# Full 128 rows in place of 64 in one score matmul of an attention stage, on one core

## The chip, the cores and the metric

The kernel runs on one core of a Trainium2 chip. The metric is the device time of one execution in microseconds (us). A core has a matrix engine (TensorE, PE in the rows; its weight loads are listed apart as PEld), VectorE (DVE), ScalarE (ACT) and GpSimd (POOL); DMA queues are issued by SyncE (SP) and others. TensorE's clock has two levels, 1.2 and 2.4 GHz; the rows give the granted clock as a share of 2.4 GHz.

## What is computed

The reference is a backbone of two layers over 512 latent tokens of width 2048, with 256 context tokens ahead of them. Layer 0 is an attention layer with two groups of heads, layer 1 a Fourier mixing layer. The part that matters here is the first group of layer 0, eight latent heads ("A"). Their queries and keys have a part of 128 without position (nope) and a part of 64 with rotary position (pe); the rotary key is shared by all heads:

```python
def mla_qk(q_nope, q_pe, k_nope, k_pe):
    b, l, h, _ = q_nope.shape
    q = jnp.concatenate([q_nope, q_pe], axis=-1)[:, :, :, None, :]
    k = jnp.concatenate([k_nope, jnp.broadcast_to(k_pe, (b, l, h, A_ROPE))], axis=-1)
    return q, k
...
        sc = jnp.einsum("bqgrd,bkgd->bgrqk", qi, k, preferred_element_type=jnp.float32) * scale
        p = jax.nn.softmax(sc, axis=-1).astype(v.dtype)
        return jnp.einsum("bgrqk,bkge->bqgre", p, v)
```

There are 512 queries (four blocks of 128) against 256 + 512 = 768 keys. The second group, eight heads with normed queries and two key heads ("B"), has no such split.

## The kernel before

All data is float32. To keep its precision, each operand of a matmul is split into a high half (rounded to the type that TensorE multiplies, fp32r) and a low half, the rest. A product is then three matmuls, high by high, high by low and low by high (mm3, lines 56 to 59); low by low is left out. A split is a cast on ScalarE and a subtraction on VectorE (lines 39 to 46). Every matmul is issued by line 54 behind a load of its weights, the stationary operand.

The stages in order are: norms and projections of the tokens, the attention of layer 0 (function attention, line 692), its output projection, and the Fourier layer. In the attention stage the order of TensorE's work is that of the code (pinned, line 900). A loop over 64 steps (line 912), one step for each head and block of 128 queries, does for step i: the projections that later heads need (fills: q_nope, k_nope, q_pe, v_a), the transposes of the softmax of step i (turn), the product with the values of step i - 2 (values), and the scores of step i + 2 (scores). Steps 0 to 31 are the A heads, 32 to 63 the B heads. From step 27 on the scores stand ahead of the transposes. The second half of k_nope stands in the late table (line 920): in an even step ahead of the value product, in an odd one behind it, so that the next head's scores follow at once. The opening (lines 908 and 909) has the same sequence: the second half of k_nope, then scores; with the three odd steps there are four such places.

One score block (function score, lines 844 to 849) makes a tile S of 128 queries by 768 keys, in two segments of 512 and 256 columns. For each segment there are five matmuls: two for the rotary part, three for the nope part. For the rotary part, the query tile st (stk in the rows; line 806) of a head has 128 rows: in one half of the rows the high half of the 64 rotary query values, in the other half the low half of the same values; for even heads the high half is in rows 0 to 63, for odd heads in rows 64 to 127. The rotary key is stored twice, in rows 0 to 63 and in rows 64 to 127, and split into self.kpe[0] (high, kpeh in the rows) and self.kpe[1] (low, kpel). The first matmul, over all 128 rows, gives (high + low) query by high key. The second takes only the 64 rows with the high query, r to r + 63, by the low key. The nope part is qh, ql by kh, kl.

Behind a score block come the maximum (VectorE), the exp (ScalarE), the reciprocal (VectorE), the scaling (GpSimd, tile pm) and, two steps later, six transposes (pt).

A product of a B head is the nope part alone, six matmuls per block with 128 rows.

Of the kernel before, what the change touches and what calls it, by code (L numbers as in the profile page):

```python
# [24 lines left out]
class Build:  # L25
# [666 lines left out]
    def attention(self, keep):  # L692
        nc, d = self.nc, self.d
        self.y_d = [self.dr.tile([128, 512], F32, name=f"y{h}") for h in range(16)]
        with ExitStack() as s:
# [25 lines left out]
            def weight(src, k, n):  # L721
                raw = rawp.tile([128, 1024], F32, name="raw")
                r = raw[:, :k * n]
                self.load(r.rearrange("p (k c) -> p k c", k=k), src)
                hi = pg.tile([128, 1024], F32R, name="pgh")
                lo = pg.tile([128, 1024], F32R, name="pgl")
                self.split(r, hi[:, :k * n], lo[:, :k * n])
                return [(hi[:, n * i:n * i + n], lo[:, n * i:n * i + n]) for i in range(k)]

            def gemm(ps, lhs, rhs):  # L730
                n = len(lhs)
                for i in range(n):
                    self.mm3(ps, lhs[i], rhs[i], i == 0, i == n - 1)
                return ps

            def cut(p, a, b):
                return p[0][:, a:b], p[1][:, a:b]

            def pair(shape, tag, bufs=2):
                return (ap.tile(shape, F32R, name=tag + "h", bufs=bufs), ap.tile(shape, F32R, name=tag + "l", bufs=bufs))  # L740
# [58 lines left out]
            parts = {}  # L799
# [31 lines left out]
            def k_nope(h, part):  # L831
                if part == 0:
                    parts["kw"] = weight(d["wkn"][h], 4, 128)
                    parts["k", h] = pair([128, 768], "k")
                w, kn = parts["kw"], parts["k", h]
                a, b = segs[part]
                ps = acc.tile([128, 512], F32, name="acc")[:, :b - a]
                gemm(ps, w, [cut(c, a, b) for c in self.ckv])
                self.split(ps, *cut(kn, a, b))
                if part == 0:  # L840
                    return
                qn, st, r, i = parts["q", h], parts["st", h // 2][h % 2], 64 * (h % 2), h % 2

                def score(ps, qt):
                    o = 128 * qt
                    for a, b in segs:
                        self.mm(ps[:, a:b], st[:, o:o + 128], self.kpe[0][:, a:b], True, False)
                        self.mm(ps[:, a:b], st[r:r + 64, o:o + 128], self.kpe[1][r:r + 64, a:b], False, False)
                        self.mm3(ps[:, a:b], cut(qn, o, o + 128), cut(kn, a, b), False, True)
                heads[h] = {"score": score, "col": 0, "v": lambda t: [v[:, t, 128 * i:128 * i + 128] for v in parts["v", h // 2]]}  # L850

# [30 lines left out]
            for hp in range(4):  # L882
                b, n = 8 * hp, hp + 1
                if hp:
                    fills[b + 1] = [(q_nope, 2 * hp + 1)]
                fills[b + 2] = [(k_nope, 2 * hp + 1, 0)]
                late[b + 2] = (k_nope, 2 * hp + 1, 1)
                if n < 4:
                    fills[b + 3] = [(q_pe, n)]
                    fills[b + 4] = [(q_nope, 2 * n)]  # L890
                    fills[b + 5] = [(k_nope, 2 * n, 0)]
                    late[b + 5] = (k_nope, 2 * n, 1)
                    for t in range(3):
                        fills[b + 6 + t] = [(v_a, n, t)]
# [807 lines left out]
```

## Time and profile before

| | us |
|---|---|
| median of three runs | 2356.12 (2350.45 to 2357.21) |
| the profiled execution | 2353.7 |
| its span, first to last instruction | 2351.9 |
| TensorE busy | 2173.0 (92%) |
| VectorE busy | 1887.2 (80%) |
| ScalarE busy | 948.2 (40%) |
| GpSimd busy | 428.3 (18%) |

In the profiled execution the first score matmul of an A head starts at 643.06 us and the last at 870.16; the B heads follow to 960. The rows further down are of four views: busy time of each engine in a stretch; instructions in order of time (start and duration); groups of instructions by operands, with their mean duration and the idle time of their engine just before them; and the page of the profile. In a name like `S<-kpel,stk 64*128 64x512` the output tile stands first, then the moving and the stationary operand, the rows by columns of the weights, and the rows by columns of the moving operand. A matmul's bar overlaps the next one's; how fast the engine goes is read from the starts.

### The profile page before, as it was taken

Reading aid. Unit: us, or ns where it says so; the run is one execution under the profiler, and the core shown is the slowest. Engines: PE = TensorE matmul, PEld = TensorE weight load, DVE = VectorE, ACT = ScalarE, POOL = GpSimd, SP = SyncE. Lnnn points to the kernel's source line nnn. Section 1 sums busy time; section 2 is a strip of 40 time slices with the busy share of each in tenths; the row PEclk is TensorE's granted clock in tenths of the full one; section 3 lists DMA queues with packets and bytes.
Section 4 is the critical chain, followed back from the end, with each engine's and each line's share of the span. In section 5 each row is a group of like instructions: output and inputs, shape, how many; then the busy total and the mean of one; then the engine's idle time right before and its main releaser. Section 6 shows DMA issues by size and latency. Waiting matters only on the chain. (4 is left out here: it accounts for less than half of the span.)

```text
span 2351.9 us, 39267 instructions
## 1 busy us (share of the span) xinstructions
PE 2173.0 (92%) x15708; PEld 1998.8 (85%) x15708; DVE 1887.2 (80%) x2603; ACT 948.2 (40%) x1321; POOL 428.3 (18%) x407
## 2 busy tenths in 40 slices
PE   5999989989899999999978898998999998998994
PEld 3779879889888889877758898998999998998994
DVE  5456799998755569677889998779998999879898
ACT  2222344433443457422464333445344435445331
POOL 1023413100111113100252222001221224002003
PEclk9999989999999999999999999999999999999997
DMA  8852344666511122588536675535555456536332
GB/s 339 311 192 100 126 164 159 202 219 203 203 42 57 59 75 71 181 294 281 184 116 224 247 276 186 174 132 187 179 174 174 164 173 214 185 127 247 130 135 116
DMA packets 128702, 412.63 MB, mean 175 GB/s; under 512 B 14852, under 2 KB 15492, under 8 KB 126728
## 3 DMA queue, kind: packets, MB, share of 16 engines
q1 hardware_dynamic: 113144, 359.04, 44.7%
q0 software_dynamic: 8320, 31.33, 3.7%
q10 hardware_dynamic: 7056, 19.76, 2.2%
q8 instruction: 123, 2.02, 0.3%
q14 instruction: 59, 0.48, 0.1%
HBM read 347.81 MB, written 62.26 MB: 174 GB/s over the span
## 5 line engine op out<-in xcount | busy, mean ns | idle before, releaser
L54 PE MATMUL r<-bth,wl 128*128 128x256 f32 x1848 | 524.3, 284 | 16.0 <-DVE wl L44 15.7
L54 PE MATMUL r<-bth,wh 128*128 128x256 f32 x1848 | 525.6, 284 | 0.0
L54 PE MATMUL r<-btl,wh 128*128 128x256 f32 x1848 | 524.3, 284 | 1.3 <-DVE btl L44 1.0
L41 ACT CAST wh<-wraw 128x1024 fp32r<-128x1024 f32 x262 | 274.7, 1050 | 395.8 <-PE r L54 284.5
L44 DVE TENSOR_TENSOR wl<-wraw,wh 128x1024 fp32r<-128x1024 f32 x262 | 336.7, 1289 | 52.5 <-ACT wh L41 52.3
L54 PEld LDWEIGHTS r<-bth,wl 128*128 128x128 f32 x1848 | 352.1, 191 | 18.5 <-DVE wl L44 18.5
L54 PEld LDWEIGHTS r<-btl,wh 128*128 128x128 f32 x1848 | 351.1, 190 | 2.1 <-DVE btl L44 1.2
L54 PEld LDWEIGHTS r<-bth,wh 128*128 128x128 f32 x1848 | 351.5, 190 | 0.5 <-issue 0.5
L41 ACT CAST wh<-ws 128x1024 fp32r<-128x1024 f32 x183 | 191.8, 1049 | 339.9 <-PE r L54 321.4
L44 DVE TENSOR_TENSOR wl<-ws,wh 128x1024 fp32r<-128x1024 f32 x183 | 229.6, 1255 | 12.2 <-ACT wh L41 10.0
L197 DVE SCALAR_TENSOR_TENSOR mac<-macraw,cs,mac 128x512 f32<-128x512 f32 x240 | 193.6, 807 | 12.4 <-DMA macraw<-in_ada 11.0
L54 PE MATMUL r<-hlh,wl 128*128 128x256 f32 (+1 forms) x480 | 148.4, 309 | 31.8 <-DVE wl L44 31.7
L54 PE MATMUL r<-hlh,wh 128*128 128x256 f32 (+1 forms) x480 | 147.2, 307 | 0.1
L54 PE MATMUL r<-hll,wh 128*128 128x256 f32 (+1 forms) x480 | 145.8, 304 | 0.0
L54 PE MATMUL r<-bah,wl 128*128 128x256 f32 x384 | 113.3, 295 | 25.3 <-DVE wl L44 25.3
L54 PEld LDWEIGHTS r<-hlh,wl 128*128 128x128 f32 x480 | 94.7, 197 | 38.6 <-DVE wl L44 35.7
L41 ACT CAST pgh<-raw 128x512 fp32r<-128x512 f32 (+2 forms) x104 | 65.9, 660 | 124.2 <-DMA raw<-in_wo 51.4
L54 PE MATMUL r<-bah,wh 128*128 128x256 f32 x384 | 112.0, 292 | 0.0
L54 PE MATMUL r<-bal,wh 128*128 128x256 f32 x384 | 111.9, 291 | 0.0
L54 PE MATMUL oacc<-pgl,yh 128*128 128x512 f32 x256 | 103.1, 403 | 8.8 <-DVE pgl L44 8.8
L54 PE MATMUL r<-bbh,wl 128*128 128x256 f32 x384 | 108.6, 283 | 2.7 <-DVE wl L44 2.7
L54 PE MATMUL r<-bcl,wh 128*128 128x256 f32 x384 | 108.6, 283 | 1.5 <-DVE bcl L44 0.9
(489 smaller groups left out, 5707.4 us busy)
## 6 DMA issues: line engine op xcount, KB each, us to landing
macraw<-in_ada SPq DMA_DIRECT2D x72, 512.0 KB, 6.3
wraw<-in_win SPq DMA_DIRECT2D x66, 512.0 KB, 7.2
raw<-in_adas SPq DMA_DIRECT2D x64, 512.0 KB, 5.6
wraw<-in_wg SPq DMA_DIRECT2D x64, 512.0 KB, 6.9
wraw<-in_wu SPq DMA_DIRECT2D x64, 512.0 KB, 4.3
wraw<-in_wo SPq DMA_DIRECT2D x64, 512.0 KB, 4.6
macraw<-in_ada SPq DMA_DIRECT2D x112, 256.0 KB, 3.9
raw<-in_wo SPq DMA_DIRECT2D x40, 512.0 KB, 4.9
```

The costliest lines, as they stand in the source:

```text
L41: ins = nc.scalar.copy(out=hi, in_=src)
L44: sub = (eng or nc.vector).tensor_sub(out=lo, in0=src, in1=hi.bitcast(F32))
L54: self.pin(self.nc.tensor.matmul(ps, lhsT=a, rhs=b, start=start, stop=stop))
L197: ins = nc.vector.scalar_tensor_tensor(out=acc, in0=raw[:, k, :], scalar=col, in1=acc, op0=ALU.mult, op1=ALU.add)
```

## The change

The second rotary matmul takes all 128 rows of st and of the low key in place of the 64 rows from r. It so adds the product of the low query half and the low key, which was left out before. The variable r goes. Nothing else is changed; the instructions of every engine stand in the same order as before.

```diff
-                qn, st, r, i = parts["q", h], parts["st", h // 2][h % 2], 64 * (h % 2), h % 2
+                qn, st, i = parts["q", h], parts["st", h // 2][h % 2], h % 2
...
                     for a, b in segs:
                         self.mm(ps[:, a:b], st[:, o:o + 128], self.kpe[0][:, a:b], True, False)
-                        self.mm(ps[:, a:b], st[r:r + 64, o:o + 128], self.kpe[1][r:r + 64, a:b], False, False)
+                        self.mm(ps[:, a:b], st[:, o:o + 128], self.kpe[1][:, a:b], False, False)
                         self.mm3(ps[:, a:b], cut(qn, o, o + 128), cut(kn, a, b), False, True)
```

## Rows read from the trace of the kernel before

**Rows 1.** The page: span of the profiled execution and its instructions.
```profile
span 2351.9 us, 39267 instructions
```

**Rows 2.** Busy time by stretch (start:end, length, engines, PEclk, DMA share, GB/s): A heads, B heads.
```profile
642.90:870.30 227.40, 227.40 (x1335) 185.88 (x1334) 127.55 (x248) 97.51 (x190) 35.60 (x40) 1.00 0.18 56
870.30:960.10 89.80, 89.80 (x681) 85.50 (x680) 79.53 (x186) 63.75 (x137) 33.23 (x40) 1.00 0.29 95
```

**Rows 3.** TensorE in order of time (start us, duration us), one score block of an A head.
```profile
705.65 0.39 PE L54 MATMUL S<-kpeh,stk 128*128 128x512 f32 x1
705.97 0.50 PE L54 MATMUL S<-kpel,stk 64*128 64x512 f32 x1
706.40 0.50 PE L54 MATMUL S<-kh,qh 128*128 128x512 f32 x1
706.74 0.40 PE L54 MATMUL S<-kl,qh 128*128 128x512 f32 x1
...
707.20 0.28 PE L54 MATMUL S<-kpeh,stk 128*128 128x256 f32 x1
707.41 0.38 PE L54 MATMUL S<-kpel,stk 64*128 64x256 f32 x1
707.72 0.39 PE L54 MATMUL S<-kh,qh 128*128 128x256 f32 x1
707.94 0.28 PE L54 MATMUL S<-kl,qh 128*128 128x256 f32 x1
...
708.19 0.28 PE L54 MATMUL acc<-pgh,ckv0h 128*128 128x256 f32 x1
```

**Rows 4.** TensorE in order of time, one score block of a B head.
```profile
872.24 0.40 PE L54 MATMUL S<-kl,qh 128*128 128x512 f32 x1
872.47 0.39 PE L54 MATMUL S<-kh,ql 128*128 128x512 f32 x1
872.70 0.28 PE L54 MATMUL S<-kh,qh 128*128 128x256 f32 x1
872.82 0.28 PE L54 MATMUL S<-kl,qh 128*128 128x256 f32 x1
...
873.06 0.82 PE L775 MATMUL pt<-ident,pm 128*128 128x128 f32 x6
```

**Rows 5.** Weight loads by operands, A heads (count, busy us, mean ns, idle before, releaser).
```profile
L54 PEld LDWEIGHTS S<-kl,qh 128*128 128x128 f32 x64 | 12.1, 189 | 0.0
...
L54 PEld LDWEIGHTS S<-kh,qh 128*128 128x128 f32 x64 | 11.9, 186 | 11.9 <-issue 7.5 <-ACT pgh L41 0.2
L54 PEld LDWEIGHTS S<-kpel,stk 64*128 64x128 f32 x64 | 11.7, 183 | 15.7 <-issue 15.7
```

**Rows 6.** TensorE in order of time, startup: narrow matmuls (psa), then full ones.
```profile
37.27 1.07 PE L301 MATMUL psa<-raw,cs 128*32 128x256 f32 x16
38.27 0.50 PE L54 MATMUL psl<-hlh,pgh 128*128 128x512 f32 x1
38.61 0.40 PE L54 MATMUL psl<-hll,pgh 128*128 128x512 f32 x1
38.85 0.40 PE L54 MATMUL psl<-hlh,pgl 128*128 128x512 f32 x1
```

**Rows 7.** All engines in order of time: a score directly behind k_nope's second half.
```profile
691.37 0.40 PE L54 MATMUL S<-kpeh,stk 128*128 128x512 f32 x1
691.49 0.83 ACT L41 CAST pgh<-raw 128x768 fp32r<-128x768 f32 x1 [1.75 <-issue]
...
693.23 0.42 DVE L44 TENSOR_TENSOR kl<-acc,kh 128x256 fp32r<-128x256 f32 x1
...
693.66 0.28 PE L54 MATMUL S<-kl,qh 128*128 128x256 f32 x1
```

**Rows 8.** All engines in order of time: a scaled softmax tile, and the transposes reading it.
```profile
863.68 0.91 POOL L761 TENSOR_SCALAR pm<-pm,rs 128x768 f32<-128x768 f32 x1 [9.34 <-DVE nb L754]
...
866.01 0.82 PE L775 MATMUL pt<-ident,pm 128*128 128x128 f32 x6
```

## The prediction

> **What bounds the kernel now.** I read the time before from the outside in. The span is 2351.9 us [rows 1]; the profiled execution took 2353.7 us with what lies around the span, and the median of the three runs shown is 2356.12, 2.4 us more. The change touches one instruction of the score product of the eight A heads, so the second view is the busy time in the stretch that holds these heads, from the first score matmul to the last, beside the stretch of the B heads behind it. In the A stretch TensorE is busy for all of the 227.40 us, VectorE for 127.55, ScalarE for 97.51, GpSimd for 35.60, the DMA share is 0.18, and the granted clock is 1.00, that is 2.4 GHz throughout [rows 2]. So nothing but TensorE sets the end of this stretch: what its instructions give up here moves everything behind it. The B stretch reads the same way (89.80 of 89.80 us), and there all score matmuls have 128 rows.
>
> But busy is not the same as fast: a matmul's bar includes its wait for the array. So the third view is the order in time, read by starts and not by bars. One query block of an A head is ten matmuls, five on 512 columns and five on 256. Their starts stand at 705.65, 705.97, 706.40 and 706.74, then at the start of the 256 part at 707.20, 707.41, 707.72, 707.94, and the next work starts at 708.19 [rows 3]. The steps are 0.32, 0.43, 0.34 and then 0.23 each in the first half; 0.21, 0.31, 0.22 and then 0.12 or 0.13 in the second. In a B head, where the form never changes, a step is 0.23 for 512 columns and 0.12 for 256 [rows 4]. The extra time thus stands around the 64-row matmul alone: before it, behind it, and once more behind the first full matmul that follows.
>
> The fourth view, weight loads grouped by operands, says how. The loads of the 64-row step (kpel,stk) take 183 ns each, hardly less than the 189 ns of a full one, and the load engine stood idle for 15.7 us before them, put down to "issue", which is time in which it waited for nothing that the trace shows. Before the full loads that follow (kh,qh) it stood idle for 11.9 us, and before kl,qh, a full load behind a full matmul, for 0.0 us [rows 5]. A load that is normally hidden under the matmul ahead of it is held until that matmul has ended, both when the row form changes from 128 to 64 and when it changes back.
>
> Is it the change of form, or something about this operand? The startup of the program has another change of form: a group of 128*32 matmuls (psa) ahead of full ones. Behind it the first full matmul at 38.27 is followed by the next at 38.61, a step of 0.34, and then by one at 38.85, a step of 0.24 [rows 6]. The 0.34 is that of a score's first full matmul too. Other operands, another narrow form, the same step: I take it that the price belongs to the change of form.
>
> **The change part by part.** Removed: 64 matmuls with 64 rows and their loads, two in each of 8 x 4 query blocks. Added: 64 with 128 rows, with the same columns. The first matmul of each group (kpeh,stk) already reads all rows of the same stk tile, and both halves of kpel are written by the one fetch ahead of the stage, so the change adds no wait for data; the order of instructions is the same on all engines, and no DMA is added or moved.
>
> What the new matmul costs: its nearest rows are the matmuls of the B heads, a full one behind a full one, 0.23 us for 512 columns and 0.12 for 256 [rows 4]. The bound on the other side is today's price, the steps around it unchanged. I take the first, since it is the same form in the same surroundings, and since a step of 0.12 with a load of 189 ns in it can only be had by loading under a running matmul.
>
> One query block then goes from 708.19 - 705.65 = 2.54 us [rows 3] to 5 x 0.23 + 5 x 0.12 = 1.75 us, which is 0.79 us less. Half of it lies in each of the two column parts (1.55 to 1.15, and 0.99 to 0.60). With 32 blocks the gain is 25.3 us, all on the engine that sets the end.
>
> What takes some of it back: work on other engines that was hidden under the slow score steps. Look at the four scores that start directly behind the second half of a k_nope. There ScalarE first casts a weight tile (pgh, at 691.49), then the key part, and VectorE follows with kl at 693.23, which ends at 693.65; the matmul that reads it (kl,qh on 256 columns) starts at 693.66 [rows 7]. It is just in time today, 2.28 us behind the score's first matmul at 691.37. With 128 rows that matmul would be due after 5 x 0.23 + 3 x 0.12 = 1.51 us, and this chain starts from the end of k_nope, not from the score, so it gets no shorter: 0.77 us of wait, taken for all four alike, 3.1 us. Between 0 (were the casts to start sooner) and 3.1 I take the whole.
>
> The other chain is the softmax: maximum, exp, reciprocal and scaling by GpSimd, then the transposes two blocks later. Where blocks follow each other most closely, near the change to the B heads, the scaled tile (863.68 + 0.91 = 864.59) is ready 1.42 us before the transposes at 866.01 that read it [rows 8]. One score block lies between, so 0.79 of that goes and 0.63 stays. I cost it at nothing; the cover is the score block itself, and if VectorE's queue has slipped by more than 0.63 us there, about 1 us is lost.
>
> Everything behind the A heads starts sooner by what is left and I see nothing there that is held by an absolute time: the weights of the output projection are fetched as attention's buffers come free, so they move along. The sum is 25.3 - 3.1 = 22.2 us. Against the profiled execution this is 2353.7 - 22.2 = 2331.5; against the median 2356.12 - 22.2 = 2333.9. I forecast **2333 us**.
>
> **The rivals.** First, new waits eat more than I counted. VectorE works in order, so a reciprocal can stand behind the maximum of a later block. If half of the 32 blocks lost the whole 0.79 us to a chain on VectorE or ScalarE, 12.6 us more would go, leaving about 9.6: 2356.1 - 9.6 = 2346.5. For it speaks the margin of 0.01 us in [rows 7]; against it that VectorE is busy for only 56% of the stretch [rows 2], and that most blocks have a projection, a transpose and a value product between a score and the reader of its result. Chance 0.08.
>
> Second, the change does not do what it says, and the step stays as slow with 128 rows: a load that shares rows with the matmul in flight is held until that has ended, and a full load shares all of them. Then all loads of a stream would be exposed, the ten steps keep their 2.54 us, and the time stays at 2356. Against it stand the steps of 0.12 us in the B heads, which are shorter than one load [rows 4, 5], and the 0.0 us before kl,qh. For it only that the step kpeh to kpel reads the same tile stk twice; but kh,qh and kl,qh share qh in the same way. Chance 0.07. The Trainium skill, "TensorE: Matmul & The Clock Gate", Part 3, under "What overlaps and what doesn't", has this rule: a weight load overlaps a running matmul only where the row groups differ. By that rule the change would bring nothing; this trace does not agree, since full loads of 189 ns lie in steps of 120 ns.
>
> Third, slower. In every engine's queue the order is the same, so a shorter matmul alone makes nothing later; what can is the clock. TensorE would now stream full rows without gaps through the A stretch. If the granted clock fell there from 1.00, work at its lower level, 1.2 GHz, would take twice as long. The stretch holds 227.4 - 22.2 = 205.2 us of work; to end 7.1 us (0.3%) later than today it must last 234.5, so 29.3 us of the work must run at the lower level, a mean granted clock of 0.875. At 0.85 the stretch lasts 241.4 and the kernel 2370. Against it: the B stretch does exactly this for 89.8 us and keeps 1.00 [rows 2]. Chance 0.03.
>
> **How the numbers follow.** My forecast has 0.82. What a measurement of this kernel can tell from no change is about 0.3%, or 7.1 us. The forecast and the first rival are both beyond that: faster 0.90. The second rival gives no change: 0.07. The third: slower, 0.03. The low end of the range is the whole gain with no wait, 25.3 us from the fastest run shown (2350.45), 2325; the high end is a gain of 15 us, the forecast with another 7 us lost as in the first rival, from the slowest (2357.21), 2342.
>
> **What would show it.** Right: the starts of the ten matmuls of a query block at steps of 0.23 and 0.12, the whole at 1.75 us; no idle time on "issue" before the loads of kpel and kh,qh; the A stretch about 205 us long at a granted clock of 1.00; a wait of some 0.8 us for kl at the four scores behind a k_nope, and nowhere else for long. Wrong: steps of 0.3 to 0.4 still around kpel (second rival), idle time of TensorE of 10 us and more on VectorE in the A stretch (first), a clock below 1.00 there (third), or a stretch behind the A heads that grew by what they lost.

## The result and the profile after

The changed kernel takes 2330.04 us (median of four runs, 2323.94 to 2335.44) against 2356.66 (2350.45 to 2360.93) beside it: a ratio of 0.9898 with a 95% interval of 0.9867 to 0.9928, that is 17 to 31 us less. The forecast was 2333.

The profiled execution after has a span of 2322.2 us, 29.7 less than [rows 1]. More than the change can give, so the first thing is to see where those 29.7 us lie. Below is the busy time by stretch: of the kernel before ahead of the A heads' first score and behind the B heads, then of the kernel after in four stretches (start:end, length, busy time of PE, PEld, DVE, ACT and POOL with instructions, granted clock, DMA share, GB/s).

```profile
0.00:643.00 643.00, 578.71 (x4226) 508.67 (x4227) 485.23 (x632) 219.84 (x293) 116.15 (x113) 0.97 0.58 202
...
960.10:2351.90 1391.80, 1277.17 (x9474) 1218.87 (x9472) 1194.95 (x1540) 567.09 (x702) 243.31 (x215) 0.97 0.54 188
```

```profile
0.00:637.00 637.00, 577.75 (x4227) 506.23 (x4228) 485.45 (x632) 219.51 (x293) 116.07 (x113) 0.98 0.59 204
637.00:841.00 204.00, 202.98 (x1332) 184.24 (x1331) 125.64 (x247) 97.18 (x190) 34.92 (x39) 1.00 0.20 62
841.00:930.50 89.50, 89.50 (x678) 85.20 (x678) 79.76 (x186) 63.22 (x135) 33.81 (x40) 1.00 0.29 94
930.50:2322.20 1391.70, 1277.35 (x9479) 1218.66 (x9477) 1195.58 (x1540) 567.10 (x704) 244.22 (x215) 0.97 0.55 188
```

The A stretch, read to the hundredth from the first score matmul (643.06 before, 636.98 after) to the next work behind the last score block (870.28 and 841.17), went from 227.22 to 204.19 us: **23.0 us less**. The B heads kept their 89.1 us (to 959.36 before, 930.26 after), and what follows them is 0.6 us shorter. The other 6 us lie ahead of the A heads, where the two programs are the same; over the eight profiles of this study whose programs are the same up to there, the A heads start anywhere from 636.98 to 645.51 us. So the change is worth 23.0 us in these two profiles, and the rest of the 29.7 is spread between executions. For that reason the experiments below are read from the A stretch, and timed only where the whole matters.

One score block after, TensorE in order of time, against [rows 3]:

```profile
693.34 0.39 PE L54 MATMUL S<-kpeh,stk 128*128 128x512 f32 x1
693.56 0.39 PE L54 MATMUL S<-kpel,stk 128*128 128x512 f32 x1
693.79 0.39 PE L54 MATMUL S<-kh,qh 128*128 128x512 f32 x1
694.02 0.40 PE L54 MATMUL S<-kl,qh 128*128 128x512 f32 x1
694.26 0.40 PE L54 MATMUL S<-kh,ql 128*128 128x512 f32 x1
694.49 0.28 PE L54 MATMUL S<-kpeh,stk 128*128 128x256 f32 x1
694.61 0.28 PE L54 MATMUL S<-kpel,stk 128*128 128x256 f32 x1
694.73 0.28 PE L54 MATMUL S<-kh,qh 128*128 128x256 f32 x1
694.85 0.28 PE L54 MATMUL S<-kl,qh 128*128 128x256 f32 x1
694.96 0.28 PE L54 MATMUL S<-kh,ql 128*128 128x256 f32 x1
695.08 0.28 PE L54 MATMUL acc<-pgh,ckv0h 128*128 128x256 f32 x1
```

Every step is 0.22 to 0.24 us for 512 columns and 0.11 to 0.12 for 256; the block takes 695.08 - 693.34 = 1.74 us, where it took 2.54. The weight loads of the A heads after, by operands (count, busy us, mean ns, idle before them), answer to [rows 5]: the idle time of 15.7 and 11.9 us is down to 1.5 and 1.3, and the full load of kpel takes 189 ns, where the half one took 183.

```profile
L54 PEld LDWEIGHTS S<-kpel,stk 128*128 128x128 f32 x64 | 12.1, 189 | 1.5
L54 PEld LDWEIGHTS S<-kh,qh 128*128 128x128 f32 x64 | 12.0, 188 | 1.3
```

What TensorE and its loads now wait for in the A stretch (waiting engine and operation, releaser, total us, times, longest), where the list before the change had 23.2 us on "issue" ahead of the score loads, and but two waits of 0.2 us for another engine:

```profile
PEld acc L54 <- DVE ld L688: 0.9, 3, 0.3
PEld acc L54 <- DVE kl L44: 0.8, 1, 0.8
PE acc L54 <- DVE kl L44: 0.6, 1, 0.6
PEld S L54 <- DVE kl L44: 0.3, 1, 0.3
```

### The profile page after: what moved, and what is told of

Read it like the earlier page. It is cut to its first block, busy times and chain, and to the rows that moved or that the text cites. A ratio compares the mean times of both kernels' runs of the same rounds, so it can differ in the third digit from the quotient of the medians.

```text
span 2322.2 us, 39267 instructions
## 1 busy us (share of the span) xinstructions
PE 2147.6 (92%) x15708; PEld 1994.3 (86%) x15708; DVE 1886.4 (81%) x2603; ACT 947.0 (41%) x1321; POOL 429.0 (18%) x407
## 4 chain that ended last, share of the span: by engine, by line
PE 35%; DVE 8%; DMA 3%; issue 3%; ACT 1%; POOL 1%; DVEq 0%; SPq 0%; ACTq 0%; POOLq 0%
PE r L54 33%; DVE wl L44 2%; DMA wraw<-in_wg 2%; PE psd L54 1%; DVE mac L197 1%; DMA stage<-yt 1%; DVE wraw L1185 1%; DVE btl L44 1%; DVE ws L1206 0%; DVE x L1539 0%; DVE c L1219 0%; PE pt L1492 0%; DVE hf L1325 0%; DVE x L1535 0%; POOL btl L44 0%
## 5 line engine op out<-in xcount | busy, mean ns | idle before, releaser
L54 PE MATMUL r<-hlh,wl 128*128 128x256 f32 (+1 forms) x480 | 147.2, 307 | 26.7 <-DVE wl L44 26.6
L54 PE MATMUL r<-bah,wl 128*128 128x256 f32 x384 | 112.7, 293 | 25.1 <-DVE wl L44 25.1
L54 PE MATMUL r<-bbh,wh 128*128 128x256 f32 x384 | 109.4, 285 | 0.0
```

Source lines behind the costliest of these rows:

```text
L54: self.pin(self.nc.tensor.matmul(ps, lhsT=a, rhs=b, start=start, stop=stop))
```

## The experiments

The theory to test: each change of the row form on TensorE, from full to narrow and back, has a price in time, whatever the operand. The rivals: the price hangs on each narrow matmul itself; on the half of the array that it stands in; on overlapping rows; on the stacked tile; on the order of the work.

### The narrow matmul back in half of the heads

In the changed kernel:

```diff
+                        r = slice(0, 128 if h % 2 else 64)
-                        self.mm(ps[:, a:b], st[:, o:o + 128], self.kpe[1][:, a:b], False, False)
+                        self.mm(ps[:, a:b], st[r, o:o + 128], self.kpe[1][r, a:b], False, False)
```

> The changed kernel with the 64-row matmul put back in the four even heads only (rows 0 to 63). Measured is the A stretch, from the first score matmul of the A heads to the next work behind their last score block: 227.2 us before, 204.2 us after the change. Theory (each change of row form holds the next weight load until the running matmul has ended, whatever the operand): the 16 blocks of the even heads take 2.53 us again, those of the odd heads stay at 1.75, the A stretch is 204.2 + 16 x 0.78 = 216.7 us. Rival (the price hangs on the half of the array that the 64 rows stand in, upper or lower): about 204 or about 227.

The A stretch runs from 640.67 to 856.48, 215.8 us (216.7 expected; the wait at the opening and the one ahead of a value product, which the 204.2 us contain, are hidden again). The blocks of the even heads take 2.53 or 2.54 us, but for two that stand directly behind transposes (2.61 and 2.62, as before the change), those of the odd heads 1.74 or 1.75 where nothing else waits. The loads of the two kinds stand side by side in one execution:

```profile
L54 PEld LDWEIGHTS S<-kpel,stk 128*128 128x128 f32 x32 | 6.0, 189 | 0.8
L54 PEld LDWEIGHTS S<-kpel,stk 64*128 64x128 f32 x32 | 5.8, 183 | 7.8 <-issue 7.8
```

Half of the narrow loads, half of the idle time (7.8 of 15.7 us). In the kernel before, the odd heads with the lower half of the array paid the same (2.52 to 2.54), so the half doesn't matter.

### Narrow matmuls kept, but side by side

In the kernel before:

```diff
                     for a, b in segs:
                         self.mm(ps[:, a:b], st[:, o:o + 128], self.kpe[0][:, a:b], True, False)
+                    for a, b in segs:
                         self.mm(ps[:, a:b], st[r:r + 64, o:o + 128], self.kpe[1][r:r + 64, a:b], False, False)
+                    for a, b in segs:
                         self.mm3(ps[:, a:b], cut(qn, o, o + 128), cut(kn, a, b), False, True)
```

> The kernel before, its 64-row matmuls kept, but the two of a block side by side: first both rotary matmuls with 128 rows, then both with 64, then the nope part of both segments. Two changes of form per block in place of four. Theory (price per change of form): one way in (0.09 us) and one way out (0.19 and 0.11) are left, a block takes 1.75 + 0.39 = 2.14 us, the A stretch 204.2 + 32 x 0.39 = 216.7 us, the whole some 11 us less than before. Rival 1 (price per 64-row matmul): 2.5 us a block, 227 us, no change of the whole. Rival 2 (a load is held when its rows overlap those of the running matmul, for narrow forms): one more held load of some 0.1 us per block, 2.25 us a block, 220 us.

The A stretch takes 860.22 - 645.51 = 214.7 us, the whole 2341.68 us against 2351.74 beside it, a ratio of 0.9952 (0.9929 to 0.9975), 6 to 17 us less with every 64-row matmul in place. TensorE in order of time (x2 is the 512 and the 256 column matmul in one row):

```profile
704.61 0.51 PE L54 MATMUL S<-kpeh,stk 128*128 128x512 f32 x2
705.05 0.61 PE L54 MATMUL S<-kpel,stk 64*128 64x512 f32 x2
705.59 0.50 PE L54 MATMUL S<-kh,qh 128*128 128x512 f32 x1
705.92 0.40 PE L54 MATMUL S<-kl,qh 128*128 128x512 f32 x1
...
706.75 0.28 PE L54 MATMUL acc<-pgh,ckv0h 128*128 128x256 f32 x1
```

The block takes 2.14 us, as expected by the price per change. Per narrow matmul it would still be 2.5. The stretch is 2.0 us shorter than expected: TensorE is busy for 214.68 of 214.70 us there, so the waits of the changed kernel, which I had built in by starting from its 204.2, are hidden again.

### The same order with full rows

The edit is the one above, made to the changed kernel.

> The order of the previous experiment with 128 rows throughout: a control for the order alone. Theory: no change of form, a block at 1.75 us, the A stretch at 204 us as after the change, within 1 us. Rival (part of the gain comes from the order in which the two PSUM segments take turns): 2 us or more away from 204.

From 643.78 to 847.96 it is 204.2 us, the same as after the change. The order alone gives nothing.

### Twice as many narrow matmuls, as many changes of form

In the kernel before:

```diff
-                        self.mm(ps[:, a:b], st[:, o:o + 128], self.kpe[0][:, a:b], True, False)
+                        self.mm(ps[:, a:b], st[r:r + 64, o:o + 128], self.kpe[0][r:r + 64, a:b], True, False)
```

> The kernel before with 64 rows in both rotary matmuls, so that the low half of the rotary query is left out; twice as many 64-row matmuls, as many changes of form as before. Theory (price per change of form): as before, 2.53 us a block and 227 us for the A stretch; the step between the two 64-row matmuls is 0.23 us (512 columns) and 0.12 (256). Rival 1 (price per 64-row matmul): two prices, 3.3 us a block, 252 us. Rival 2 (a load is held when its rows overlap those of the running matmul): a step of 0.33 and 0.21 between the two, 2.7 us a block, 233 us.

The A stretch takes 868.38 - 641.46 = 226.9 us (227 expected, 252 and 233 by the rivals). But the step between the two narrow matmuls was not what I wrote. TensorE in order of time, the value product ahead of the block in the first line:

```profile
703.82 0.28 PE L54 MATMUL acc<-pth,vl 128*128 128x256 f32 x1
704.03 0.50 PE L54 MATMUL S<-kpeh,stk 64*128 64x512 f32 x1
704.37 0.39 PE L54 MATMUL S<-kpel,stk 64*128 64x512 f32 x1
704.69 0.50 PE L54 MATMUL S<-kh,qh 128*128 128x512 f32 x1
705.02 0.39 PE L54 MATMUL S<-kl,qh 128*128 128x512 f32 x1
705.25 0.40 PE L54 MATMUL S<-kh,ql 128*128 128x512 f32 x1
705.58 0.38 PE L54 MATMUL S<-kpeh,stk 64*128 64x256 f32 x1
```

The step into the first narrow matmul is 0.21 (0.12 for 256 columns without a change), the one from it to the second is 0.34 and not 0.23, the one back to full rows 0.32 and not 0.43, and the next 0.33. The sum is right and the split was wrong: **each change of form costs about 0.10 us on the step into it and 0.10 us on the step after it**. With one narrow matmul alone, as in the kernel before, the second half of the way in and the first half of the way out fall on the same step, which is the 0.43 of [rows 3]. A block counted from its first score matmul takes 2.44 us and not 2.53, as 0.09 us of the way in now fall on the step ahead of it. The step of 0.34 alone would also fit a load held by overlapping rows; the total of 226.9 and the grouped kernel, where that rival wanted 2.25 us a block, don't. Nor does the load of the second narrow matmul, which stands in the same 64 rows as the first: it starts 0.23 us ahead of its matmul at 704.37, under the first one.

```profile
704.14 0.19 PEld L54 LDWEIGHTS S<-kpel,stk 64*128 64x128 f32 x1
```

### The full matmul taken out

```diff
-                        self.mm(ps[:, a:b], st[:, o:o + 128], self.kpe[1][:, a:b], False, False)
```

> The changed kernel with the product of query and low rotary key left out altogether: four matmuls of 128 rows per segment. It measures what the full matmul itself costs in place. Theory (a full matmul costs only its columns, and TensorE still sets the end): 0.23 + 0.12 = 0.35 us less per block, 11.2 us in 32 blocks, some of it lost to new waits; the A stretch 193 to 195 us. Rival (by now other engines' chains set the end of the stretch): 199 us or more.

The A stretch takes 839.16 - 643.34 = 195.8 us, 8.4 less than after the change. Where nothing waits, a block takes 1.40 us, that is 0.35 less than 1.75: the full matmul costs its columns and nothing else. Over 32 blocks that would be 11.2 us; 2.8 of them went to new waits, more than the theory allowed for (193 to 195), less than the rival said (199 or more). The two largest waits of TensorE's loads there:

```profile
PEld acc L54 <- DVE ld L688: 2.0, 3, 0.7
PEld S L54 <- DVE kl L44: 1.4, 5, 0.6
```

The waits of a score for kl, one after the change, are five here: with 11.2 us more taken from the scores, VectorE's chains show more.

### A narrow matmul where there was none

In the B heads of the changed kernel:

```diff
-                        self.mm3(ps[:, a:b], cut(qb, o, o + 128), cut(kb, a, b), True, True)
+                        self.mm(ps[:, a:b], qb[0][:, o:o + 128], kb[0][:, a:b], True, False)
+                        self.mm(ps[:, a:b], qb[0][0:64, o:o + 128], kb[1][0:64, a:b], False, False)
+                        self.mm(ps[:, a:b], qb[1][:, o:o + 128], kb[0][:, a:b], False, True)
```

> The changed kernel with a 64-row matmul put where there was none: in the B heads the middle one of the three matmuls of a segment (query high, key low) takes rows 0 to 63 only, so half of that product is left out. The A heads stay as after the change. Theory (the price belongs to the change of row form, not to the rotary operands): each B segment gains one way in and one way out, 0.39 us, 32 blocks x 0.78 = 25 us; the stretch of the B heads grows from 89.5 us to 114 us, a block of six matmuls from 1.05 to 1.83 us. Rival (the price belongs to the tile with high and low halves stacked, or to using one stationary tile twice): the stretch stays at 90 us.

The stretch of the B heads grows from 89.1 us (841.17 to 930.26 after the change) to 114.3, 25.2 us more where 25 were expected, at a clock of 1.00; a block grows to 1.83 us, with less arithmetic in it than before. The busy time of that stretch (columns as above) and one block of it, TensorE in order of time, against [rows 4]:

```profile
845.05:959.37 114.32, 114.32 (x675) 86.34 (x673) 82.74 (x187) 67.10 (x136) 34.25 (x41) 1.00 0.24 78
```

```profile
850.34 0.40 PE L54 MATMUL S<-kh,qh 128*128 128x512 f32 x1
850.66 0.50 PE L54 MATMUL S<-kl,qh 64*128 64x512 f32 x1
851.09 0.50 PE L54 MATMUL S<-kh,ql 128*128 128x512 f32 x1
851.43 0.28 PE L54 MATMUL S<-kh,qh 128*128 128x256 f32 x1
851.64 0.38 PE L54 MATMUL S<-kl,qh 64*128 64x256 f32 x1
851.95 0.38 PE L54 MATMUL S<-kh,ql 128*128 128x256 f32 x1
852.17 0.82 PE L775 MATMUL pt<-ident,pm 128*128 128x128 f32 x6
```

The steps of 0.32, 0.43, 0.34 and 0.21, 0.31, 0.22 are those of [rows 3] to the hundredth, with other operands. That settles that the price belongs to the change of row form and not to the rotary tile.

### The startup's narrow groups in pairs

In the changed kernel, the call ada(j, 0) is moved directly ahead of ada(j, 1), and ada(j, 2) directly ahead of ada(j, 3) (lines 383 to 408):

```diff
                     outer(k, 0, 0)
-                    ada(j, 0)
...
                     outer(k, 0, 2, 3)
+                    ada(j, 0)
                     ada(j, 1)
...
-                    ada(j, 2)
                     outer(k, 0, 0)
+                    ada(j, 2)
                     ada(j, 3)
```

> The changed kernel with the narrow groups of the startup (psa, 128*32) put side by side in pairs from the second block on: about 28 groups become 14, and 14 ways in (0.10 us) and 14 ways out (0.11 us) go. Theory (price per change of form, also for narrow columns): about 3 us less until the A heads start, where the startup is bound by TensorE. Rival (the later group delays the loads that its tiles gate, and the startup's DMA share of 0.85 has no room): no gain or a loss, more waits of psa for its raw tiles.

The last product of the startup starts at 154.8 us after the change and at 151.4 here, 3.4 us sooner (grouped by operands: count, minimum, median and maximum ns, first and last start; the changed kernel, then this one):

```profile
L54 PE MATMUL psl<-hlh,pgh x64: 387/478/775, 32.1 to 154.8; 128*128 128x512 f32 x64
```

```profile
L54 PE MATMUL psl<-hlh,pgh x64: 387/437/775, 32.4 to 151.4; 128*128 128x512 f32 x64
```

The median bar of this product fell from 478 to 437 ns: 18 of the 64 stood directly behind a narrow group, 7 do here. In the eight profiles with the startup as it was, the last product starts between 154.2 and 159.4 us, and between 154.8 and 155.1 in the three of them whose granted clock up to there was 1.00, as it is here. So 151.4 lies below all eight, and more than 3 us below those at an equal clock: a price is paid around the 128*32 groups too, and pairs pay it less often.

These groups differ from the products around them in their columns and also in type, plain float32 and not fp32r. A product in plain float32 over the full 128*128 (line 211), among fp32r products of the kernel before, shows that it is not the type. Its two passes start at 321.55 and 321.98, 0.43 us apart:

```profile
321.98 0.59 PE L211 MATMUL psm<-mac,ones 128*128 128x512 f32 x1
...
322.52 0.28 PE L54 MATMUL r<-hll,wh 128*128 128x256 f32 x1
322.65 0.28 PE L54 MATMUL r<-hlh,wl 128*128 128x256 f32 x1
```

From the second pass to the second product behind it, 0.55 us go by, one pass of 0.43 and one step of 0.12; nothing is added.

The whole took 2329.88 us, a ratio of 0.9895 (0.9866 to 0.9924) to the kernel before: 3.4 us are too little to be told from 0.9898.

### The opening reordered as well

```diff
             k_nope(0, 0)
-            v_a(0, 0)
             k_nope(0, 1)
+            v_a(0, 0)
             scores(0)
```

> The changed kernel with the startup's narrow groups in pairs, as in the experiment before, and with the opening of the attention reordered: the second half of k_nope ahead of the value projection, so that the first score no longer stands directly behind it. Theory (the 0.34 us that the load of kl,qh waits for kl in the first score block is work hidden before the change; given more room it is hidden again): the first block falls from 2.16 to about 1.76 us, the A stretch from 204.2 to about 203.8; the startup again some 3 us shorter than after the change; the whole 2326 us, which differs from 2330 by less than the runs spread. Rival (the first score waits for something else, the casts of the weights): the first block stays at 2.1 us.

The first score block takes 1.75 us in place of 2.16, the A stretch 845.78 - 642.20 = 203.6 us in place of 204.2, and the startup's last product starts at 153.4, again sooner than in any of the eight, though the granted clock up to there was 0.94. The wait at the opening was kl's. The whole took 2327.58 us, a ratio of 0.9884 (0.9868 to 0.9901) to the kernel before; the ratio is the lowest here, but its interval overlaps that of the change alone.

## Why the prediction was right, point by point

- **TensorE alone sets the end of the A stretch.** Right: it lost 23.0 us, and what lies behind it moved along, with its length kept to 0.6 us.
- **0.79 us per block, 25.3 us in all.** Right. Blocks without a wait went from 2.53 to 1.745 us, 0.785 x 32 = 25.1 us. The price of a full matmul was taken from the B heads, the same form in the same surroundings, and the experiment that took the matmul out gave the same 0.35 us a block.
- **The price belongs to the change of form.** Right, and now shown on other operands; for narrow columns a price of the same kind is shown at the startup. The reading "held until the running matmul has ended" was half of it: that is the 0.10 us on the step into the new form. The other 0.10 us on the step after it I had seen only behind the way out, not on the way in. Nor do the rows show what the load is held for: the bars' ends are modelled, and at 705.97 the bar of the matmul before (705.65 + 0.39) had not ended [rows 3].
- **3.1 us given back at four scores behind a k_nope, all for kl.** The size was near by luck, the places were wrong. 25.1 - 23.0 = 2.1 us were given back, but only the opening has the wait that I described: the first block takes 2.16 us, 0.41 too long. At the three odd steps I had misread who reads the key, in the section on the kernel too, where the next head's scores are said to follow at once. The score that follows there is the last block of the head before; the new key is for the next step, with a whole step's work between. That kl ended at 693.65 and a kl,qh started at 693.66 [rows 7] was chance, since the two are not the same head's, and I took a small gap for a dependency without following the names through the loop. What was given back instead: three times 0.38 us where a query projection waits for its accumulator until VectorE has finished the rotary product of q_pe (ld L688), 0.27 us in the wait and 0.11 on the step behind it, and 0.60 us before a value product (829.54), put down to a kl that reads an accumulator. With the opening that makes 2.1 us. Neither was costed.
- **The softmax chain keeps 0.63 us.** Right: the scaled tile of the same block is ready at 837.06 after the change, 0.64 us before the transposes at 837.70, and no wait for pm appears in the A stretch.
- **The rivals.** More waits: 2.1 us, not the 15.7 of that case (3.1 + 12.6). A load that shares rows is held whatever its form: refuted by the full steps of 0.12 us after the change. By the rule of the Trainium skill that the prediction names ("TensorE: Matmul & The Clock Gate", Part 3, "What overlaps and what doesn't") the stretch would have kept its 227 us; it took 204.2, so these runs do not agree. The clock: it stayed at 1.00 in both stretches.
- **The whole.** 22.2 us were forecast; 26.6 lie between the medians, 24 by the ratio (17 to 31), 23.0 in the stretch. The stretch is the closer measure of the change; what the whole shows beyond it is within the spread of the part ahead of the A heads, which the range had to take in and did.

## What to carry to other kernels

Look at the starts of matmuls, not at their bars: a lone matmul with 64 rows in a stream of full ones cost more here than a full one. If its operands can be filled up to the full form with data that do no harm, as here the low-by-low product that had been left out, fill them up; if they can't, put the narrow ones side by side, since the price was paid per change and not per matmul. And before a wait is costed from two times that lie close together, check that the one really reads what the other writes.

## What the runs showed of the hardware

- A change between 128 and 64 rows on TensorE at a clock of 1.00 costs about 0.10 us on the step into the new form and 0.10 us on the next. A narrow matmul of 256 columns alone among full ones thus adds 0.39 us to a stream in which its own step is 0.12.
- The traces show where the second part comes from: at a change the load of the new form and its matmul start together, where in a uniform stream a load starts one step sooner (in the kernel after at 638.26 for the matmul at 638.38). All engines in order of time, the kernel before:

```profile
643.38 0.18 PEld L54 LDWEIGHTS S<-kpel,stk 64*128 64x128 f32 x1 [0.25 <-issue]
643.38 0.50 PE L54 MATMUL S<-kpel,stk 64*128 64x512 f32 x1
```

  The same stands in the kernel after at the opening, where no form changes and the load waits for kl:

```profile
638.80 0.19 PEld L54 LDWEIGHTS S<-kl,qh 128*128 128x128 f32 x1 [0.34 <-DVE kl L44]
638.80 0.39 PE L54 MATMUL S<-kl,qh 128*128 128x256 f32 x1
...
639.02 0.28 PE L54 MATMUL S<-kh,ql 128*128 128x256 f32 x1
...
639.14 0.28 PE L54 MATMUL acc<-pgh,ckv0h 128*128 128x256 f32 x1
```

  The step from 638.80 to 639.02 is 0.22 us and not 0.12. So in these rows the second 0.10 us goes with a load that could not start ahead of its matmul, whatever held it. That the matmul's step then holds a part of its own load is my reading. Why a change of form holds the load at all stays open.
- The same program reached its A heads between 636.98 and 645.51 us. The mean granted clock up to there was 0.98 where it was soonest, but 0.96 where it was latest and 0.95 at 643.78, so the clock alone does not order these times. What spreads them is not settled here.
